# Output weights of the second layer split in halves, and two steps of waiting work behind each memory query

## The chip, the cores and the metric

The kernel runs on one core of one Trainium2 chip. The metric is the device time of one execution in microseconds; runs of the kernel before gave 899.07, 900.21 and 903.23 us, so the median is 900.21 us. A core has five engines that work side by side, each through its own list of instructions in a fixed order: TensorE (PE in the profile; its weight loads are PEld), VectorE (DVE), ScalarE (ACT), GpSimd (POOL) and SyncE (SP, which issues the loads). They wait for each other by semaphores. An instruction that waits holds up everything behind it on its engine.

## The reference

One inference step of a decoder trunk with two layers, for 256 prompt tokens and 8 single-token samples with shared weights (model width 2048). What matters for the second layer, cut down:

```
q, f, iv, mq, g = split(h @ w_in)            # 12 heads q/f/iv, 4 memory queries mq, 16 gate blocks g
fg  = lb + (1 - lb) * sigmoid(f)             # HGRN2: gated linear recurrence
o   = chunked_recurrence(silu(q), 1 - fg, iv, log(fg))   # per head, causal, with a state
mix = o * rsqrt(mean(o*o) + eps) * norm_w    # 12 blocks of 128
p   = softmax(mq @ mem_k.T / sqrt(128))      # 4 memory heads; prompt: one shared memory,
mem = p @ mem_v                              #   samples: each its own cached memory
y   = (concat(mix, mem) * silu(g)) @ w_out
out = layer_norm(alpha * h + y)
```

Everything is float32 at the interface.

## The kernel before

Each float32 operand of a large product is split into a high and a low float16 part, and a product is three matmuls (high x high, high x low, low x high; `passes`, L302 to L306). Activations lie transposed: 128 partitions of the width, 264 tokens in the free dimension (256 of the prompt, 8 samples).

All weights and cached memories pass through one **stream** (class `Stream`). A unit of the stream is a block of 128 x 2048 float32, 1 MB. Three things happen to it: SP loads it into one of 4 `raw` buffers (L80); `prep` splits it into one of 4 `hl` buffers, ACT writing the high part (L98) and DVE the low part (L99); then the unit's function runs its matmuls. Unit 4 onwards of the first layer's units is split in one piece of 2048 columns; units whose number is in `stream.halved` are split in two pieces of 1024, each with an instruction on ACT and one on DVE. In the kernel before, the set holds the 2048-column units of the second layer up to the last gate, and not the 16 blocks of output weights, which are added to the stream after it is computed.

Beside the units there is waiting work: generators in the queue `side`, run a step at a time by `pump`. After each unit the function `after` calls `pump(1)`. The last recurrence generator (`hg_side`, ten steps for a pair of heads) and then four memory-head generators (`memp_side`, two steps each) are in that queue while the second layer's last units pass: 4 memory queries (`mq`), then the samples' memory keys (`ck_unit`, 4 units) and values (`cv_unit`, 4 units) between the gate blocks `g`, then the 16 output blocks `o`.

The names that the texts use, with their lines:

- `rms` (L1183) is the last matmul of a recurrence head; ACT takes its logarithm and exponential (L1184, L1187, a table load before each), DVE then scales the head (L1190) and the gate follows (L729 on DVE, L730 on ACT, L731 on DVE). L734 and L735 make the gate itself from `g`.
- Memory heads of the prompt: scores `msc` (PE), maximum on DVE (L612, L613), exponential on ACT (L615), reciprocal and scaling on DVE (L616, L618), transposes `mpt` (L623 on PE), split into `mphl` (L250 on ACT for the high part, L252 on DVE for the low part), product `mpo` (PE), copy to `mix` (L635).
- Samples: score columns `mss` over the four `ck` units, then `mems_soft`: transposes `mrow` (L667 on PE), maximum (L671, L672 on DVE), exponential (L673 on ACT), reciprocal and scaling (L674, L675 on DVE), transposes `mback` (L678 on PE), split into `msphl` (L250 on ACT, L252 on DVE), and the products `mso` (L697, L698 on PE) over the four `cv` units.
- Output: `proj` into a PSUM bank `o`, residual L748 on DVE, square L760 on ACT, sums L765 and L766 on DVE. The last eight output blocks are split into `held` buffers of their own and are used twice: for 176 tokens first, for the other 88 at the end.

PSUM banks are shared by tag, two buffers each: `sc` for the scores and `rms`, `pt` for all transposes (`mpt`, `mrow`, `mback`), `pj` for gates and outputs. A buffer is given out anew when its last reader is through, in the order in which the program asks. The program asks for a bank when a generator's step or a unit runs, so `pump` also sets the order in which banks change hands. A scheduler then arranges the instructions of each engine; the result is a fixed order per engine.

Of the kernel before, what the change touches and what calls it, by code (L numbers as in the profile page):

```python
# [31 lines left out]
NM = 4  # L32
# [103 lines left out]
def trunk_kernel(  # L136
# [42 lines left out]
    stream = Stream(nc, cp, 4, 4)  # L179
# [34 lines left out]
    def small_work():  # L214
        with ExitStack() as behind:
            for first in (*stream.settled, first_mm[0]):
                behind.enter_context(tc.issue_after(first.ins))
            small_ops()
# [66 lines left out]
    def pump(n):  # L285
        for _ in range(n):
            while side:
                try:
                    next(side[0])
                    break  # L290
                except StopIteration:
                    side.popleft()
            if not side:
                return

    def drain():
        while side:
            for _ in side.popleft():
                pass
# [8 lines left out]
    def proj(hl, src, n, name, cols=slice(None), tag="pj"):  # L308
        w = hl.rearrange("p s (c f) -> p s c f", c=NC)
        pt = bank(tag, 2, name)  # L310
        for c in range(NC):
            passes(pt[:, :n], lambda s: w[:, s, c], lambda s: src[:, s, c, cols], c == 0, c == NC - 1)
        return pt[:, :n]
# [11 lines left out]
    def spread_bias(g):  # L325
        dst = bass.AP(tensor=l_d.tensor, offset=l_d.offset + g * 32 * 287, ap=[[LROW, 24], [288, 32], [1, 287]])
        src = l_t[:, 96 - 32 * g : 383 - 32 * g].unsqueeze(1).to_broadcast([24, 32, 287])
        nc.gpsimd.dma_start(dst, src)
# [47 lines left out]
    def v_rows(p):  # L376
        f = slice(p * P, (p + 1) * P)
        pt = bank("pt", 2, f"vt{p}")
        for n in range(2):
            nc.tensor.transpose(pt[:, n * P : (n + 1) * P], vf[:, p, n * P : (n + 1) * P], ident)  # L380
        nc.tensor.transpose(pt[:TS, 256:384], vf[:, p, TP:T], ident)
        src = pt[:, :256].rearrange("p (n f) -> p n f", n=2)
        split_from(vhl[:, 0, :, f], vhl[:, 1, :, f], src, SA)
        nc.vector.tensor_copy(vsn[:, f], pt[:TS, 256:384])
# [178 lines left out]
    def mq_unit(h):  # L563
        def fn(hl):
            pt = proj(hl, xhl, T, f"mq{h}")
            split_from(mqhl[:, 0, h], mqhl[:, 1, h], pt, 1.0 / SW)

        return fn
# [152 lines left out]
    def gate_fin(l):  # L721
        a, j = fin[l].popleft()
        while j not in done[l]:
            pump(1)
        assert (("swa" if l == 0 else j) if j < NQ else "mem") in done[l]
        gate_by(a, mix[:, j], j)
# [6 lines left out]
    def silu2(out, pt):  # L733
        nc.scalar.activation(out, pt, AF.Tanh, scale=0.5 * CP)  # L734
        nc.vector.scalar_tensor_tensor(out, out, 1.0, pt, op0=ALU.add, op1=ALU.mult)  # L735
# [4 lines left out]
    def out_part(l, i, hl, cols, tag="pj", first=False):  # L740
        n = len(range(*cols.indices(T)))
        pt = proj(hl, bhl, n, f"o{l}{i}_{cols.start}", cols, tag)
        with tc.high_priority(400) if first else nullcontext():
            residual(l, i, cols, n, pt)
# [23 lines left out]
    def out_unit(l, i):  # L768
        def fn(hl):
            if i == 0:  # L770
                drain()
                while fin[l]:
                    gate_fin(l)
                for s in range(2):
                    acc[s] = cp.tile([P, T], F32, tag="mphl", name=f"acc{l}{s}", bufs=2)
            if l == 0 or i < NC - NSPLIT:
                out_part(l, i, hl, slice(0, T))
            else:
                held[i] = hl
                out_part(l, i, hl, slice(0, TA))  # L780
            if i == NC - 1:
                if l == 0:
                    side.append(layer_norm())
                else:
                    finish_tokens()

        return fn
# [37 lines left out]
    def layer_norm():  # L825
        def homes(k):
            tags = ("mean", "sil", 3), ("rstd", "sil", 3), ("r0", "sq", 2)
            return [cp.tile([P, T], F32, tag=tag, name=f"{n}{k}", bufs=bufs) for n, tag, bufs in tags]

        mean, rstd = norm_factors(0, slice(0, T), homes)  # L830
        for i in range(NC):
            z = xres[:, i]
            w, b = ln_scalars(0, i)
            tc.keep_in_program_order(nc.vector.tensor_tensor(z, z, mean, op=ALU.subtract))
            tc.keep_in_program_order(nc.vector.scalar_tensor_tensor(z, z, w, rstd, op0=ALU.mult, op1=ALU.mult))
            nc.scalar.activation(z, z, AF.Identity, bias=b)
            split_from(xhl[:, 0, i], xhl[:, 1, i], z, SA)
            if i % 2 == 1:
                yield
        yield  # L840
# [70 lines left out]
    def wb(w, i):  # L911
        return w[i].rearrange("p c f -> p (c f)")
# [97 lines left out]
    def hq_unit(h):  # L1010
        def fn(hl):
            p1 = H["p"]
            pt = proj(hl, xhl, T, f"hq{h}")
            if h % 2 == 0:
                cur["q"] = p1.tile([P, 2, T], F32, tag="hq", name=f"hqs{h}", bufs=2)
            silu2(cur["q"][:, h % 2], pt)
            if h % 2 == 1:
                side.append(hg_side(h // 2, cur["q"], cur["vn"], cur["fg"], cur["qk"]))

        return fn  # L1020
# [31 lines left out]
    def early_gate(j):  # L1052
        def fn(hl):
            silu2(mix[:, j], proj(hl, xhl, T, f"g1{j}"))

        return fn
# [190 lines left out]
    n_first = len(stream.units)  # L1247
    for pi in range(HD // 2):
        for part, unit in (("f", f_unit), ("v", hv_unit)):
            for i in range(2):  # L1250
                stream.add(wb(w_in1, NB1[part] + 2 * pi + i), unit(2 * pi + i))
        for h in (2 * pi, 2 * pi + 1):
            stream.add(wb(w_in1, NB1["q"] + h), hq_unit(h))
            state_at[h] = len(stream.units)
            stream.add(state[pi][:, (h % 2) * TS * P : (h % 2 + 1) * TS * P], state_unit(h), SA, whole=True)
            if h < NG1:
                stream.add(wb(w_in1, NB1["g"] + h), early_gate(h))
    for h in range(NM):
        stream.add(wb(w_in1, NB1["mq"] + h), mq_unit(h))

# [6 lines left out]
    def g1(j):  # L1267
        stream.add(wb(w_in1, NB1["g"] + j), gate_unit(1, j))
# [5 lines left out]
            g1(late.popleft())  # L1274
    while late:
        g1(late.popleft())
    whole_w = {i for i in range(n_first, len(stream.units)) if stream.units[i][0].shape[1] == 2048}
    stream.halved = whole_w
    for i in range(NC):
        stream.add(wb(w_o[1], i), out_unit(1, i), home=hold if i >= NC - NSPLIT else None)  # L1280

    def after(i):
        if i == 1:
            small_work()
        if i == 4:
            for p in range(2):
                v_rows(p)
        if 1 <= i < 3:
            spread_bias(2 * i - 2)
            spread_bias(2 * i - 1)  # L1290
        pump(1)
        for rows in due:
            rows()
        due[:], later[:] = later, []

    stream.run(after)
    l2.close()

# [138 lines left out]
```

## Time and profile before

| what | us |
|---|---|
| median of 3 runs | 900.21 (899.07 to 903.23) |
| the profiled execution | 900.73 |
| its span (first to last instruction) | 898.9 |
| PE busy in the span | 884.6 (98%) |
| DVE busy | 703.3 (78%) |
| ACT busy | 587.7 (65%) |

How to read it: 1.8 us of the profiled execution's time lie around its span. A PE matmul's end is modelled: one of 264 columns is drawn with about 0.28 us, though the next starts 0.11 us later, so a real pause of PE looks some 0.17 us shorter in busy and idle times than it is between the starts of two matmuls. The second layer's part that the change touches begins with the four memory queries at about 710 us; the samples' memory lies between 732 and 780 us, the first output block starts at 792.7 us, the last weights are split at about 845 us.

### The profile page before, as it was taken

To read this page: it belongs to the slowest core of one execution; us is meant where nothing else is said; L and a number is where in the kernel's file an instruction comes from. 1 tells how busy PE (TensorE), PEld (TensorE's weight loads), DVE (VectorE), ACT (ScalarE), POOL (GpSimd) and SP (SyncE) were. 2 spreads that over 40 slices of the span, in tenths; PEclk is the share of its full clock that TensorE was granted. 3 is DMA by queue.
4 is the path that set the end of the run, shared out by engine and by line. 5 is a ranking of instruction groups with operands and counts; after the bars stand their busy time and mean duration, and the time that the engine had idled before them with its cause. 6 is when DMAs were issued, how large, how long until landed. Compare 5 with 4: busy or idle time off the path is not lost.

```text
span 898.9 us, 21938 instructions
## 1 busy us (share of the span) xinstructions
PE 884.6 (98%) x9281; PEld 761.1 (85%) x9281; DVE 703.3 (78%) x1294; ACT 587.7 (65%) x1046; POOL 34.9 (4%) x68
## 2 busy tenths in 40 slices
PE   9999999999999999999999999999999999999996
PEld 6888889678888888875888888888888988888896
DVE  7869877669886666697598798978879999878736
ACT  6757776657664433476767777768779676957415
POOL 1100010000000000002000000000000000000000
PEclk9999999999999999999999999999999999999999
DMA  9998566557795555556474553835446678666303
GB/s 348 385 355 320 191 244 201 188 209 270 253 333 204 200 187 191 192 207 223 148 273 152 214 212 130 307 134 217 178 183 233 238 279 302 227 234 253 124 2 98
DMA packets 37854, 198.68 MB, mean 221 GB/s; under 512 B 4555, under 2 KB 10732, under 8 KB 17532
## 3 DMA queue, kind: packets, MB, share of 16 engines
q1 hardware_dynamic: 33024, 181.55, 55.5%
q0 software_dynamic: 4688, 15.67, 4.6%
q8 instruction: 72, 1.18, 0.5%
q14 instruction: 26, 0.21, 0.1%
q10 hardware_dynamic: 44, 0.07, 0.1%
HBM read 180.03 MB, written 17.22 MB: 219 GB/s over the span
## 4 chain that ended last, share of the span: by engine, by line
PE 81%; DVE 11%; ACT 4%; issue 2%; DMA 1%; ACTq 0%; DVEq 0%
PE o L304 5%; PE o L306 5%; PE o L305 5%; PE g L304 5%; PE g L306 5%; PE g L305 5%; DVE hl L99 5%; PE q L304 2%; PE q L306 2%; PE q L305 2%; PE hv L304 2%; PE hv L306 2%; PE hv L305 2%; PE hq L305 2%; PE hq L304 2%
## 5 line engine op out<-in xcount | busy, mean ns | idle before, releaser
L99 DVE SCALAR_TENSOR_TENSOR hl<-raw,hl 128x1024 f16<-128x1024 f32 (+2 forms) x232 | 365.0, 1592 | 68.4 <-ACT hl L98 68.0
L98 ACT ACTIVATE hl<-raw 128x1024 f16<-128x1024 f32 (+2 forms) x232 | 305.0, 1344 | 87.8 <-PE o L306 47.0
L305 PEld LDWEIGHTS <-hl 128*128 128x128 f16 (+2 forms) x2048 | 197.3, 98 | 30.8 <-issue 2.5
L304 PEld LDWEIGHTS <-hl 128*128 128x128 f16 (+2 forms) x2048 | 197.4, 98 | 30.1 <-ACT xhl L250 1.2
L306 PEld LDWEIGHTS <-hl 128*128 128x128 f16 (+2 forms) x2048 | 197.3, 98 | 28.6 <-DVE hl L99 0.3
L306 PE MATMUL g<-xhl,hl 128*128 128x264 f16 x512 | 141.4, 276 | 0.0
L305 PE MATMUL g<-xhl,hl 128*128 128x264 f16 x512 | 141.4, 276 | 0.0
L304 PE MATMUL g<-xhl,hl 128*128 128x264 f16 x512 | 141.3, 276 | 0.0
L304 PE MATMUL o<-mix,hl 128*128 128x264 f16 x384 | 105.5, 276 | 2.2 <-DVE xres L748 1.8
L306 PE MATMUL o<-mix,hl 128*128 128x264 f16 x384 | 105.8, 276 | 0.0
L305 PE MATMUL o<-mix,hl 128*128 128x264 f16 x384 | 105.8, 276 | 0.0
L304 PE MATMUL q<-xhl,hl 128*128 128x264 f16 x192 | 53.0, 276 | 0.0
L304 PE MATMUL hv<-xhl,hl 128*128 128x264 f16 x192 | 53.0, 276 | 0.0
L305 PE MATMUL hq<-xhl,hl 128*128 128x264 f16 x192 | 53.0, 276 | 0.0
L306 PE MATMUL hq<-xhl,hl 128*128 128x264 f16 x192 | 53.0, 276 | 0.0
L304 PE MATMUL hq<-xhl,hl 128*128 128x264 f16 x192 | 53.0, 276 | 0.0
L305 PE MATMUL q<-xhl,hl 128*128 128x264 f16 x192 | 53.0, 276 | 0.0
L306 PE MATMUL hv<-xhl,hl 128*128 128x264 f16 x192 | 53.0, 276 | 0.0
L306 PE MATMUL q<-xhl,hl 128*128 128x264 f16 x192 | 53.0, 276 | 0.0
L305 PE MATMUL hv<-xhl,hl 128*128 128x264 f16 x192 | 53.0, 276 | 0.0
L305 PE MATMUL f<-xhl,hl 128*128 128x264 f16 x192 | 52.9, 276 | 0.0
L306 PE MATMUL f<-xhl,hl 128*128 128x264 f16 x192 | 52.8, 276 | 0.0
(338 smaller groups left out, 1856.1 us busy)
## 6 DMA issues: line engine op xcount, KB each, us to landing
raw<-in_w_in SPq DMA_DIRECT2D x88, 1024.0 KB, 5.6
raw<-in_w_o SPq DMA_DIRECT2D x32, 1024.0 KB, 4.8
raw<-in_w_mk SPq DMA_DIRECT2D x8, 1024.0 KB, 4.9
raw<-in_w_mv SPq DMA_DIRECT2D x8, 1024.0 KB, 4.9
raw<-in_c_mk SPq DMA_DIRECT2D x8, 1024.0 KB, 4.9
raw<-in_c_mv SPq DMA_DIRECT2D x8, 1024.0 KB, 4.9
raw<-in_state SPq DMA_DIRECT2D x12, 512.0 KB, 4.6
out_ss<-raw POOLq DMA_DIRECT2D x12, 512.0 KB, 2.9
```

Of the source, the lines that this page charges most:

```text
L98: hi = self.nc.scalar.activation(hl[:, 0, s], raw[:, s], AF.Copy, scale=scale)
L99: lo = self.nc.vector.scalar_tensor_tensor(hl[:, 1, s], raw[:, s], scale, hl[:, 0, s], op0=ALU.mult, op1=ALU.subtract)
L304: mm(out, lhs(0), rhs(0), start=start, stop=False)
L305: mm(out, lhs(0), rhs(1), start=False, stop=False)
L306: return mm(out, lhs(1), rhs(0), start=False, stop=stop)
```

## The change

Two edits. First, behind each of the four memory-query units of the second layer (`twos` holds their numbers) `pump` runs two steps of the waiting work where it ran one. Second, `stream.halved` is computed after the 16 output blocks have been added, so these are split in two pieces of 1024 columns as well.

```
+    twos = range(len(stream.units), len(stream.units) + NM)
     for h in range(NM):
         stream.add(wb(w_in1, NB1["mq"] + h), mq_unit(h))
...
-    whole_w = {i for i in range(n_first, len(stream.units)) if stream.units[i][0].shape[1] == 2048}
-    stream.halved = whole_w
     for i in range(NC):
         stream.add(wb(w_o[1], i), out_unit(1, i), home=hold if i >= NC - NSPLIT else None)
+    stream.halved = {i for i in range(n_first, len(stream.units)) if stream.units[i][0].shape[1] == 2048}
...
-        pump(1)
+        pump(2 if i in twos else 1)
```

What the scheduler makes of it stands below at three places. The first is PE around `mback`, the transposes that bring the samples' softmax back. Before, they stand in the middle of a gate block (the one for block 12 of the branch):

```order
L306 MATMUL g_10972<-xhl,hl_10762 128x264
L304 LDWEIGHTS hl_10762
L304 MATMUL g_10972<-xhl,hl_10762 128x264
L678 MATMUL mback_10814<-ident,mrows_10806 128x32 x2
L305 LDWEIGHTS hl_10762
L305 MATMUL g_10972<-xhl,hl_10762 128x264
L306 LDWEIGHTS hl_10762
```

Now (`mrow` stands 15 matmuls ahead of `mback`, right behind the third memory head's scores):

```order
L305 MATMUL mpo_10735<-mphl_10732,mvhl 128x256
L306 LDWEIGHTS mvhl
L306 MATMUL mpo_10735<-mphl_10732,mvhl 128x256
L678 MATMUL mback_10874<-ident,mrows_10866 128x32 x2
L623 MATMUL mpt_10880<-ident,ms_10806 128x128 x4
L697 LDWEIGHTS hl_10743
L697 MATMUL mso_10982<-msphl_10877,hl_10743 128x2
L698 LDWEIGHTS hl_10743
```

The gate blocks 11, 12 and 13 now all stand ahead of it on PE; behind it come all four units of sample values (`mso`) together with the rest of the memory heads, and then the gate blocks 14 and 15. Before, two of the values' units stood behind gate block 12 and two behind block 13. Between the last `rms` and the third head's scores `msc` PE now has 54 matmuls of gates and 12 of scores.

The second place is DVE behind the last recurrence heads. Before:

```order
L252 SCALAR_TENSOR_TENSOR msphl_10817<-mback_10814,msphl_10817 128x64
L1190 SCALAR_TENSOR_TENSOR mix<-osb_9824,small_t,osq_10758 128x264
L1190 SCALAR_TENSOR_TENSOR mix<-osb_9824,small_t,osq_10760 128x264
L612 TENSOR_REDUCE mnm_10894<-msc_10892 128x2
L729 SCALAR_TENSOR_TENSOR sil_10744<-sil_10744,mix 128x264
L729 SCALAR_TENSOR_TENSOR sil_10886<-sil_10886,mix 128x264
L613 TENSOR_SCALAR mnm_10894<-mnm_10894 128x2
L612 TENSOR_REDUCE mnm_11029<-msc_11027 128x2
```

Now, from the same heads up to the first two heads' maxima:

```order
L729 SCALAR_TENSOR_TENSOR sil_10952<-sil_10952,mix 128x264
L99 SCALAR_TENSOR_TENSOR hl_11031<-raw_10748,hl_11031 128x1024
L612 TENSOR_REDUCE mnm_10673<-msc_10671 128x2
L99 SCALAR_TENSOR_TENSOR hl_11031<-raw_10748,hl_11031 128x1024
L735 SCALAR_TENSOR_TENSOR sil_11087<-sil_11087,g_11038 128x264
L612 TENSOR_REDUCE mnm_10807<-msc_10805 128x2
L731 TENSOR_TENSOR mix<-sil_10799,mix 128x264
L731 TENSOR_TENSOR mix<-sil_10952,mix 128x264
L613 TENSOR_SCALAR mnm_10673<-mnm_10673 128x2
L613 TENSOR_SCALAR mnm_10807<-mnm_10807 128x2
```

and from there to the samples' split:

```order
L612 TENSOR_REDUCE mnm_11095<-msc_11093 128x2
L99 SCALAR_TENSOR_TENSOR hl_11110<-raw_10827,hl_11110 128x1024
L672 TENSOR_SCALAR mrnm_10867<-mrnm_10867 32x1
L99 SCALAR_TENSOR_TENSOR hl_11110<-raw_10827,hl_11110 128x1024
L735 SCALAR_TENSOR_TENSOR sil_11221<-sil_11221,g_11172 128x264
L613 TENSOR_SCALAR mnm_11095<-mnm_11095 128x2
L252 SCALAR_TENSOR_TENSOR mphl_10732<-mpt_10727,mphl_10732 128x512
L616 RECIPROCAL mz_10961<-mz_10961 128x2
L674 RECIPROCAL mrz_10868<-mrz_10868 32x1
L618 TENSOR_SCALAR ms_10959<-ms_10959,mz_10961 128x256 x2
L675 TENSOR_SCALAR mrows_10866<-mrows_10866,mrz_10868 32x256
L252 SCALAR_TENSOR_TENSOR msphl_10877<-mback_10874,msphl_10877 128x64
```

Before, the samples' split `msphl` is ahead of the last recurrence heads (L1190) on DVE, and with it the whole samples' softmax; now it is behind them and behind the first head's split `mphl`. Ahead of the first `mphl` now stand the splits of both remaining units of sample values (`hl_11031`, `hl_11110`).

The third place is DVE among the output blocks, at the residuals of the sixth and seventh block (L748). Before:

```order
L99 SCALAR_TENSOR_TENSOR held_11909<-raw_11672,held_11909 128x2048
L766 TENSOR_TENSOR acc_11438<-acc_11438,sq_0_11724 128x264
L99 SCALAR_TENSOR_TENSOR held_11968<-raw_11735,held_11968 128x2048
L748 SCALAR_TENSOR_TENSOR xres<-xres,o_0_11737 128x264
L99 SCALAR_TENSOR_TENSOR held_12025<-raw_11794,held_12025 128x2048
L765 TENSOR_TENSOR acc_11437<-acc_11437,xres 128x264
L748 SCALAR_TENSOR_TENSOR xres<-xres,o_0_11796 128x264
```

Now:

```order
L748 SCALAR_TENSOR_TENSOR xres<-xres,o_0_11755 128x264
L99 SCALAR_TENSOR_TENSOR held_12051<-raw_11814,held_12051 128x1024
L99 SCALAR_TENSOR_TENSOR held_12110<-raw_11875,held_12110 128x1024 x2
L765 TENSOR_TENSOR acc_11445<-acc_11445,xres 128x264
L766 TENSOR_TENSOR acc_11446<-acc_11446,sq_0_11805 128x264
L99 SCALAR_TENSOR_TENSOR held_12169<-raw_11936,held_12169 128x1024
L748 SCALAR_TENSOR_TENSOR xres<-xres,o_0_11816 128x264
```

The sixth block's residual (`o_0_11737`, now `o_0_11755`) stood behind the split of the fifth held block and now stands behind it and the first half of the sixth (`held_12051`); the seventh's stood behind the sixth held block and now stands behind the seventh and half of the eighth.

## The prediction

> **What bounds the kernel now.** I read the page's busy line and its chain of work first:
>
> ```profile
> span 898.9 us, 21938 instructions
> PE 884.6 (98%) x9281; PEld 761.1 (85%) x9281; DVE 703.3 (78%) x1294; ACT 587.7 (65%) x1046; POOL 34.9 (4%) x68
> PE 81%; DVE 11%; ACT 4%; issue 2%; DMA 1%; ACTq 0%; DVEq 0%
> ```
>
> TensorE is the bound: busy for 98% of the span, and 81% of the chain that ended last. No matmul is added or taken away, so the change can win only time in which PE pauses, and can lose only by new pauses. The next view, busy time by stage, says how much there is to win. I cut it where the chain of waits has its steps on other engines:
>
> ```profile
> 720.00:770.00 50.00, 49.71 (x620) 43.81 (x618) 43.60 (x70) 36.73 (x55) 0.54 (x1) 1.00 0.78 289
> 784.00:798.00 14.00, 14.00 (x127) 12.36 (x126) 14.00 (x21) 9.21 (x18) 0.00 (x0) 1.00 0.88 343
> 798.00:802.00 4.00, 3.17 (x26) 2.22 (x24) 3.61 (x9) 2.78 (x8) 0.00 (x0) 1.00 0.77 256
> 834.00:838.00 4.00, 2.24 (x27) 1.90 (x25) 4.00 (x5) 2.24 (x2) 0.00 (x0) 1.00 0.98 393
> 838.00:890.00 52.00, 52.00 (x823) 50.91 (x821) 28.68 (x70) 18.14 (x45) 0.00 (x0) 1.00 0.10 32
> 890.00:898.90 8.90, 1.49 (x6) 0.61 (x4) 4.03 (x12) 2.98 (x9) 1.65 (x4) 0.88 0.28 96
> ```
>
> After the length of the stage come PE, its weight loads, DVE, ACT and GpSimd, then the granted clock. PE has two pauses that the change could reach, one at 798 to 802 us (0.83 us idle) and one at 834 to 838 us (1.76 us idle). DVE is busy 14.00 of 14.00 us just ahead of the first and 4.00 of 4.00 around the second: where PE waits, it waits for a DVE that is full. The timeline of PE shows the true size of the first pause:
>
> ```profile
> 798.07 0.28 PE L305 MATMUL o<-mix,hl 128*128 128x264 f16 x1
> 798.18 0.28 PE L306 MATMUL o<-mix,hl 128*128 128x264 f16 x1
> 798.48 0.27 PE L304 MATMUL mpo<-mphl,mvhl 128*128 128x256 f16 x1
> 799.21 0.27 PE L304 MATMUL o<-mix,hl 128*128 128x264 f16 x1 [0.45 <-ACT mix L730]
> 799.70 0.27 PE L305 MATMUL mpo<-mphl,mvhl 128*128 128x256 f16 x1 [0.22 <-DVE mphl L252]
> ...
> 800.46 0.28 PE L304 MATMUL o<-mix,hl 128*128 128x264 f16 x1
> 800.87 0.27 PE L304 MATMUL mpo<-mphl,mvhl 128*128 128x256 f16 x1
> ```
>
> Two starts of undisturbed matmuls lie 0.11 us apart (798.07, 798.18). What exceeds that is 0.19 + 0.62 + 0.38 + 0.30 = 1.5 us: the memory heads' last transposes and splits are late when the first output block begins. For the second pause DVE and PE read:
>
> ```profile
> 834.52 2.29 DVE L99 SCALAR_TENSOR_TENSOR held<-raw,held 128x2048 f16<-128x2048 f32 x1
> 836.73 0.43 DVE L748 SCALAR_TENSOR_TENSOR xres<-xres,o 128x264 f32<-128x264 f32 x1
> 837.20 0.27 PE L304 MATMUL o<-mix,hl 128*128 128x264 f16 x1 [1.76 <-DVE xres L748]
> ```
>
> PE's eighth output block waits for a PSUM bank, which the sixth block's residual (L748) frees, and that stood behind a 2.29 us split. Everything that the change can win is thus 1.5 + 1.9 us, or 3.4 us of 900.
>
> **The moved work.** The order shows that the two extra steps move more than themselves. The memory heads now ask for their PSUM banks ahead of the samples' softmax, and so `mrow`, `mback` and all of `mso` fall behind the heads' scores and the first split. PE's list between the last `rms` and the third head's scores holds only gates and scores, and behind them a row of small steps, each of which goes to DVE and ACT and back. I lay that stretch out by hand, with the durations of the stage 755 to 805 us:
>
> ```profile
> L99 DVE SCALAR_TENSOR_TENSOR hl<-raw,hl 128x1024 f16<-128x1024 f32 x15 | 17.8, 1223 | 0.4 <-ACT hl L98 0.4
> L731 DVE TENSOR_TENSOR mix<-sil,mix 128x264 f16<-128x264 f32 x7 | 2.9, 433 | 1.0 <-ACT mix L730 1.0
> L252 DVE SCALAR_TENSOR_TENSOR mphl<-mpt,mphl 128x512 f16<-128x512 f32 x4 | 2.8, 693 | 0.0
> L612 DVE TENSOR_REDUCE mnm<-msc 128x2 f32<-128x512 f32 x4 | 2.7, 685 | 0.0
> L735 DVE SCALAR_TENSOR_TENSOR sil<-sil,g 128x264 f32<-128x264 f32 x6 | 2.5, 425 | 0.0
> L618 DVE TENSOR_SCALAR ms<-ms,mz 128x256 f32<-128x256 f32 x8 | 2.4, 351 | 0.0
> L1190 DVE SCALAR_TENSOR_TENSOR mix<-osb,small_t,osq 128x264 f32<-128x264 f32 x2 | 0.9, 489 | 4.1 <-ACT osq L1187 4.1
> L613 DVE TENSOR_SCALAR mnm<-mnm 128x2 f32<-128x2 f32 x4 | 0.7, 165 | 0.0
> L671 DVE TENSOR_REDUCE mrnm<-mrow 32x1 f32<-32x256 f32 x1 | 0.4, 403 | 0.0
> L675 DVE TENSOR_SCALAR mrows<-mrows,mrz 32x256 f32<-32x256 f32 x1 | 0.3, 342 | 0.0
> ...
> L98 ACT ACTIVATE hl<-raw 128x1024 f16<-128x1024 f32 x14 | 14.0, 1047 | 0.0
> L615 ACT ACTIVATE ms<-msc,mnm 128x256 f32<-128x256 f32 x8 | 3.7, 473 | 0.3 <-DVE mnm L613 0.3
> L250 ACT ACTIVATE mphl<-mpt 128x512 f16<-128x512 f32 x4 | 2.4, 589 | 0.0
> L734 ACT ACTIVATE sil<-g 128x264 f32<-128x264 f32 x5 | 1.9, 380 | 0.1
> L615 ACT ACTIVATION_READ_ACCUMULATOR ms<-msc,mnm 128x1 f32 x8 | 1.7, 207 | 0.0
> ```
>
> The means are full lengths; back to back an instruction starts before the last one ends, as three splits show:
>
> ```profile
> 757.89 3.50 DVE L99 SCALAR_TENSOR_TENSOR hl<-raw,hl 128x1024 f16<-128x1024 f32 x3
> 767.94 0.61 PE L1183 MATMUL rms<-osq,ones_rms 128*128 128x264 f32 x2
> 770.84 0.90 DVE L1190 SCALAR_TENSOR_TENSOR mix<-osb,small_t,osq 128x264 f32<-128x264 f32 x2 [4.11 <-ACT osq L1187]
> ```
>
> (3.50 - 1.22) / 2 = 1.14, so I take 0.09 us off each that has a follower. L729 is of L731's form and gets its length; L616, L672 and L674 are of L613's size.
>
> *First wait, third head's scores.* They need the `sc` bank of the first head, which ACT's exponential frees. From the second `rms` to L1190 on DVE it takes 770.84 - 767.94 = 2.90 us, and ACT's steps between them are the same now. Then DVE's rows as they now stand: L1190 twice 0.80, L729 twice 0.68, L99 1.14, L612 0.60, L99 1.14, L735 0.34, L612 0.60, L731 twice 0.68, L613 twice 0.25: 6.2 us. The first head's two exponentials with their read-outs are 0.47 + 0.21 twice, less four overlaps, about 1.0. Sum 10.1 us behind `rms`. PE has meanwhile the two passes of `rms` (0.44 us), 54 gate and 12 score matmuls at 0.11 us: 7.7 us. PE waits **2.4 us**.
>
> *Second, the first head's product, high part.* Call the start of the third scores T. PE has 18 small matmuls to the first `mpo`: T + 2.0. ACT has the second head's exponentials 1.0, two splits 1.9, L734 0.3 and L250 0.6: T + 3.7. PE waits **1.7 us**.
>
> *Third, its low part on DVE.* DVE has the third head's maximum at T + 0.9 (six score matmuls and a handover), and then L612 0.60, L616 0.07, L671 0.31, L613 0.08, L618 twice 0.52, L612 0.60, L99 1.14, L672 0.07, L99 1.14, L735 0.34, L613 0.08, L252 0.69: T + 6.5. PE was let go at T + 3.7 for one matmul: it waits **2.7 us**.
>
> *The rest.* DVE then has 1.0 us up to L675 (L616, L674, L618 twice, L675), PE 0.55 us of `mpo`: 0.45 us at `mback`. The split of `mback` on both engines has only four transposes as cover: 0.4 us. The second and third heads' splits come each behind a pair of weight splits for gate blocks 14 and 15, with the values' matmuls as cover: from 0 to 1.1 us, I take 0.7. Together **1.55 us**.
>
> New pauses: 2.4 + 1.7 + 2.7 + 1.55 = 8.35 us. Bounds: if the two pieces of L99 in the first wait and the two in the third were ready to run elsewhere, each wait would be 2.3 us shorter and 8.35 become 3.7; if each of the five handovers between engines costs 0.4 us more than I allow, it is 10.35.
>
> What goes: the 1.5 us at 798 us, since the memory heads are through before gate block 14. This stage is 8.35 - 1.5 = +6.85 us. Behind the stalled instructions on PE stand the two last gates and all output blocks, so nothing else can fill the time. The loads of the values' units and of gates 14 and 15 cost nothing more: SP issues them as buffers come free, and they have these 8 us in addition. If that cover were gone, a late 1 MB load would show as a wait of ACT's L98 for DMA.
>
> **The split output weights.** DVE: three halves in a row give 1.14 for each that has a follower, so a block takes 2 x 1.14 instead of 2.29 - 0.09 = 2.20, or 0.08 us more, 1.3 us for 16 blocks, spread over the 50 us of the output stage in which DVE has gaps. The halves let DVE begin one half earlier behind ACT and put a residual between two halves. But in the new order the sixth residual stands behind half a split more than before, and the seventh behind one and a half more. Take the sixth: without new loads' delay it comes 1.14 us later by the longer row and about 1 us earlier because ACT's and DVE's halves overlap. Bounds: the whole 1.9 us at 834 us goes, or a second wait of the same size comes at the next bank, +1.9. The rows are nearest to no change; I take 0.
>
> The page "Perfetto Trace Analysis" of the Trainium skill, section "Optimizing Scalar/DVE Operations", says that larger operations help where such an engine is saturated, and that breaking instructions up lets work be done sooner where it is not saturated but holds up others. By its second half the 1.9 us would go and the sum be 4.95; by its first, with DVE full for 4.00 of 4.00 us here, nothing is won.
>
> **Sum.** 6.85 + 0 on the profiled execution's span of 898.9 us gives 905.75, with the 1.83 us around it 907.6 us. That execution was 0.5 us above the median; on the median the forecast is 900.21 + 6.85 = **907.1 us**.
>
> **The rivals.**
>
> *The stretch stays hidden (not slower).* The place is the first wait. It decides when DVE's stretch from L1190 to the last L613 is shorter than what PE has: 6.2 must fall under 7.7 - 2.9 - 1.0 = 3.8 us. If the splits of the values' unit ran in the 4.1 us in which DVE idled ahead of L1190 (its row says so), 2.3 us would leave the stretch, the first wait would be near 0 and the second and third begin 2.3 us earlier. In the same way the third would lose its 2.3. What is left of the second and the rest are about 2.0 us of new pauses, if the high part's two splits are done early as well, against 1.5 to 3.4 gone: 898.8 to 900.7 us, say 899.8. For it: the idle 4.1 us are there. Against: the new order puts L99 behind L1190 on DVE, and an engine does not overtake.
>
> *Half of it.* One of the two pairs of splits is out of the way or the output stage gains its 1.9 us: 907.1 - 2.3 to 907.1 - 4.2, about 903.5 us. For it: the pause at 834 us is one of DVE's granularity. Against: the residuals' places.
>
> *The clock falls.* In the second and third wait together PE would do one matmul in 4.5 us. A lower granted clock is seen in the last row by stage (0.88 with PE busy 1.49 of 8.90 us) and not at 834 to 838 us (1.00 with 2.24 of 4.00). If it falls here, the matmuls that follow take twice their 0.11 us. With 0.88 over 8.9 us some 2.1 us were at half clock there; the 48 matmuls of a gate block would pay up to 5.3 us. The time would be 908 to 912 us, say 910. The page "TensorE: Matmul & The Clock Gate" of the Trainium skill, section "Part 1: The HAM clock gate (the "warmup" mystery)", puts the fall at one idle window of about 3.4 us, and my third wait alone is shorter than that; second and third together are longer, with a matmul between them.
>
> *The output stage pays too.* A second bank wait of 1.9 us, and none of the first gone: 907.1 + 1.9 = 909.0 us. For it: both residuals stand further back. Against: halves let ACT and DVE overlap more.
>
> **How the numbers follow.** The forecast's mechanism, with 3.7 to 10.35 us of new pauses less 1.5 at the outside, has 0.68; half of it 0.13; hidden 0.09; the clock 0.05; the output stage as well 0.05. Its own range is 903.5 to 909.2 us. The likeliest is 907.1. For 8 of 10 I reach down into the second rival and up into the last two: 902.0 to 910.0 us. What a measurement can tell from no change is about 0.5%, here 4.5 us: 895.7 to 904.7. Slower than that: of the 0.68 some 0.59, all of the last two, a fifth of the half case, 0.72 together. Faster by over 4.5 us would need more than the 3.4 us that are there: 0.03. No difference: 0.25.
>
> **What would show it.** Right: in the profile after, PE's waits name `msc`, `mpo` (high part from ACT, low part from DVE) and `mback`, in sum 6 to 9 us between 765 and 795 us, and nothing at the first output block; DVE shows L99 between the first head's L612 and L613. The first output block begins about 7 us later than 792.7. The stage of the last ten blocks is as before, DVE full, a bank wait of 0 to 3 us at a residual. Wrong: PE busy throughout the stretch; the samples' softmax waiting for nothing; a granted clock under 1.00 in it; or a pause of over 4 us among the output blocks, which would say that loads, not the row on DVE, set that stage.

## The result and the profile after

The changed kernel takes 909.43 us (median of 4 runs, 908.59 to 909.87), the kernel before 899.83 us on the same chips: a ratio of 1.0107, 95% interval 1.0093 to 1.0122, so 9.6 us slower. The forecast was 907.1 us with a range of 902.0 to 910.0. The page of its profiled execution (909.87 us):

```profile
span 908.1 us, 21972 instructions
PE 890.3 (98%) x9281; PEld 765.2 (84%) x9281; DVE 705.9 (78%) x1310; ACT 590.3 (65%) x1062; POOL 35.0 (4%) x68
PE 86%; DVE 8%; ACT 4%; issue 1%; ACTq 0%
```

PE is drawn busy 890.3 us instead of 884.6, with the same 9281 matmuls. That cannot be waiting, since waiting is not busy: some matmuls ran longer. Busy time by stage shows which (columns as in the prediction; the granted clock is the third number from the end):

```profile
765.00:775.00 10.00, 10.00 (x88) 8.56 (x86) 5.03 (x9) 7.39 (x13) 0.00 (x0) 1.00 0.44 161
775.00:785.00 10.00, 4.54 (x25) 3.17 (x23) 7.95 (x22) 6.18 (x18) 0.00 (x0) 0.80 0.31 105
785.00:795.00 10.00, 9.72 (x138) 8.13 (x138) 7.48 (x16) 7.66 (x15) 0.00 (x0) 0.50 0.41 131
795.00:805.00 10.00, 10.00 (x98) 8.32 (x97) 8.88 (x14) 6.81 (x12) 0.00 (x0) 0.84 0.99 383
835.00:845.00 10.00, 10.00 (x92) 8.70 (x91) 10.00 (x13) 8.10 (x9) 0.00 (x0) 1.00 0.98 385
```

Three things are to be seen. From 775 to 785 us PE does 25 matmuls in 10 us: the new waits. From 777 to 798 us the granted clock is at half for much of the time (0.80, 0.50, 0.84): the rival to which I gave 0.05. And at 835 us, where PE had paused 1.76 us before, it is busy throughout with DVE just as full. The waits in PE's timeline:

```profile
775.31 0.28 PE L306 MATMUL g<-xhl,hl 128*128 128x264 f16 x1
777.81 0.37 PE L304 MATMUL msc<-mkhl,mqhl 128*128 128x256 f16 x1 [2.22 <-ACT ms L615]
777.97 0.42 PE L305 MATMUL msc<-mkhl,mqhl 128*128 128x256 f16 x1
778.19 0.42 PE L306 MATMUL msc<-mkhl,mqhl 128*128 128x256 f16 x1
782.18 0.27 PE L304 MATMUL mpo<-mphl,mvhl 128*128 128x256 f16 x1 [0.69 <-ACT mphl L250]
785.27 0.37 PE L305 MATMUL mpo<-mphl,mvhl 128*128 128x256 f16 x1 [2.83 <-DVE mphl L252]
```

They stand where the hand replay put them, third scores, first product, its low part, and name ACT, ACT and DVE as forecast. Measured from start to start, less 0.11 us for the matmul itself, they are 2.39, 0.85 and 2.99 us; 0.24 us follow at `mback`. And score matmuls now start 0.21 us apart (777.97, 778.19), where the same ones start 0.11 us apart in the kernel before. DVE's timeline in the same stretch is the row that the prediction added up:

```profile
770.49 0.90 DVE L1190 SCALAR_TENSOR_TENSOR mix<-osb,small_t,osq 128x264 f32<-128x264 f32 x2 [4.97 <-ACT osq L1187]
771.99 1.22 DVE L99 SCALAR_TENSOR_TENSOR hl<-raw,hl 128x1024 f16<-128x1024 f32 x1
773.73 1.21 DVE L99 SCALAR_TENSOR_TENSOR hl<-raw,hl 128x1024 f16<-128x1024 f32 x1
776.49 0.23 DVE L613 TENSOR_SCALAR mnm<-mnm 128x2 f32<-128x2 f32 x2
...
781.81 1.21 DVE L99 SCALAR_TENSOR_TENSOR hl<-raw,hl 128x1024 f16<-128x1024 f32 x1
783.01 1.20 DVE L99 SCALAR_TENSOR_TENSOR hl<-raw,hl 128x1024 f16<-128x1024 f32 x1
784.55 0.67 DVE L252 SCALAR_TENSOR_TENSOR mphl<-mpt,mphl 128x512 f16<-128x512 f32 x1
```

From L1190 to the last L613 it is 776.72 - 770.49 = 6.23 us; I had 6.2. While DVE waited 4.97 us ahead of it, the pieces of L99 stood behind it in DVE's order. The first output block starts at 808.25 us.

**One thing about the comparisons.** The first 100 us differ by chance from one execution to the next, in instructions that all these kernels have in common: the first memory query of the second layer starts between 702.9 and 705.7 us in the profiles (703.6 in the kernel before, not at about 710 as the text ahead of the prediction has it), and the timed runs of the kernel before alone go from 898.1 to 903.2 us. So beside the medians I compare, in each profile, the stretch from the first memory query to the end of the span: 195.29 us before, 204.48 us after, 9.19 us more.

### The profile page after: what moved, and what is told of

It reads as the page before. It is cut to its first block, busy times and chain, and to the rows that moved or that the text cites. A ratio compares the mean times of both kernels' runs of the same rounds, so it can differ in the third digit from the quotient of the medians.

```text
span 908.1 us, 21972 instructions
## 1 busy us (share of the span) xinstructions
PE 890.3 (98%) x9281; PEld 765.2 (84%) x9281; DVE 705.9 (78%) x1310; ACT 590.3 (65%) x1062; POOL 35.0 (4%) x68
## 4 chain that ended last, share of the span: by engine, by line
PE 86%; DVE 8%; ACT 4%; issue 1%; ACTq 0%
PE o L306 6%; PE o L304 6%; PE o L305 6%; PE g L304 6%; PE g L305 5%; PE g L306 5%; DVE hl L99 4%; PE q L306 2%; PE q L304 2%; PE q L305 2%; PE hv L306 2%; PE hv L305 2%; PE hv L304 2%; PE hq L305 2%; PE hq L304 2%; PE hq L306 2%
## 5 line engine op out<-in xcount | busy, mean ns | idle before, releaser
L99 DVE SCALAR_TENSOR_TENSOR hl<-raw,hl 128x1024 f16<-128x1024 f32 (+2 forms) x240 | 365.1, 1540 | 67.9 <-ACT hl L98 67.0
```

Of the source, the lines that this page charges most:

```text
L99: lo = self.nc.vector.scalar_tensor_tensor(hl[:, 1, s], raw[:, s], scale, hl[:, 0, s], op0=ALU.mult, op1=ALU.subtract)
```

## The experiments

The table has all runs. "Rest" is that stretch, from one profile each. Each ratio is to runs of the kernel before on the same chip; their medians lie between 899.38 and 900.21 us.

| kernel | median us | ratio to before (95% interval) | rest, us |
|---|---|---|---|
| before | 899.83 | | 195.29 |
| after | 909.43 | 1.0107 (1.0093 to 1.0122) | 204.48 |
| halves alone | 900.56 | 1.0012 (1.0001 to 1.0023) | 193.82 |
| halves alone, again | 899.72 | 0.9996 (0.9982 to 1.0009) | 194.59 |
| two steps alone | 909.19 | 1.0113 (1.0096 to 1.0130) | 203.81 |
| softmax in another bank | 899.70 | 1.0001 (0.9990 to 1.0011) | 193.94 |
| matmuls in the waits | 908.53 | 1.0102 (1.0079 to 1.0124) | 200.79 |
| two extra steps | 899.23 | 0.9992 (0.9980 to 1.0005) | 193.97 |
| three extra steps | 910.45 | 1.0108 (1.0087 to 1.0128) | 204.53 |
| four low pieces left out | 906.52 | 1.0065 (1.0047 to 1.0082) | 200.50 |
| wide matmuls among narrow | 909.85 | 1.0110 (1.0089 to 1.0132) | 204.57 |

**The halves alone.**

```
-        pump(2 if i in twos else 1)
+        pump(1)
```

> Only the output weights are split in halves; one step of waiting work behind every memory query, as before. First theory (the moved steps carry the whole loss, and the halves by themselves end the 1.9 us bank wait among the output blocks): 899.8 - 1.9 = 897.9 us, the stretch from 760 to 800 us as before, no wait on the residual. Second reading (that wait went only because the output blocks began later and found their splits done): 899.8 us, with the wait still there. Rival (the halves carry part of the loss through a fuller DVE): 902 us or more.

The loss is gone. The rest is 1.5 us shorter than before, and the wait on the residual has shrunk from 1.8 to 0.2 us (waits of PE, total us, times, longest):

```profile
PE o L304 <- DVE xres L748: 0.2, 1, 0.2
```

The median does not show it: 900.56 us. In the profile the first memory query came 2.07 us later than before; whether the other runs began late too is not known, since they left no profile. So the same kernel ran again:

> The kernel with the halves alone once more. In its first profile it took 193.8 us from the first memory query to the end (before: 195.3) but 2.1 us more up to the first memory query, in instructions that are the same as before. If that late start was chance: about 898 us and 0.9985 of the time before. If it comes with this kernel: 900.5 us again, with the first memory query at about 705.7 us.

This time the first memory query came at 703.0 us, so the late start was chance. The rest was 0.7 us shorter than before, and the median, 899.72 us, missed the 898 that I expected. The residual's wait is not gone but smaller by an amount that varies:

```profile
PE o L304 <- DVE xres L748: 0.7, 1, 0.7
```

In both profiles a wait of 0.5 us at `mpt` (L623, on DVE's L618) has come in, which the kernel before doesn't have. The halves are worth 0.7 to 1.5 us in the profiles, and nothing that the medians can tell.

**The two steps alone.** The set of halved units is computed ahead of the output blocks, as in the kernel before:

```
+    whole_w = {i for i in range(n_first, len(stream.units)) if stream.units[i][0].shape[1] == 2048}
+    stream.halved = whole_w
     for i in range(NC):
         stream.add(wb(w_o[1], i), out_unit(1, i), home=hold if i >= NC - NSPLIT else None)
-    stream.halved = {i for i in range(n_first, len(stream.units)) if stream.units[i][0].shape[1] == 2048}
```

> Only the two steps behind each memory query; output weights split in one piece. First theory: the waits at the third head's scores (2.4 us), at the first head's product (0.8 and 3.0 us) and the half clock behind them stay as in the changed kernel; 909.4 us if the later start of the output blocks had removed the 1.9 us bank wait, 911.3 us if the halves had. Rival (the halves carry part of the loss): 906 us or less.

909.19 us, the whole loss. PE's waits:

```profile
PE mpo L305 <- DVE mphl L252: 2.7, 1, 2.7
PE msc L304 <- ACT ms L615: 2.2, 1, 2.2
PE mpo L304 <- ACT mphl L250: 1.4, 1, 1.4
```

There is no wait on L748 here either, though the output weights are split in one piece. So the moved steps alone end that wait too, and the halves alone shorten it. The likely reason here is that the output blocks begin 14.5 us later and find more of their splits done; no run shows that by itself.

The granted clock fell only once here ahead of the tail, at 783.74 us. Busy time of PE in the three stretches ahead of that (then clock, DMA share and GB/s):

```profile
773.50:776.91 3.41, 1.76 (x16) 1.00 0.35 82
776.91:780.32 3.41, 2.18 (x18) 1.00 0.54 226
780.32:783.74 3.42, 0.27 (x1) 1.00 0.00 0
```

It stayed up behind the first wait, fell behind the second and third together, and was at half for 13.65 us.

**The samples' softmax in another bank.** Both edits stay; `mrow` and `mback` go into free columns of the bank in which the samples' scores stand (in both layers).

```
-        pr = bank("pt", 2, f"mrow{l}")
+        pr = mst["s"][:, 128:384]
...
-        pb = bank("pt", 2, f"mback{l}")
+        pb = mst["s"][:, 384:]
```

> The changed kernel, with mrow and mback written into free columns of the bank of the samples' scores (mss), so that the samples' softmax needs no bank of the transposes. First theory (the order in which banks were asked for put the samples' softmax, and with it all of the samples' values, behind the heads' scores): the softmax is early again, the values' units stand among gates 12 and 13, no wait over 1 us and a granted clock of 1.00 between 770 and 790 us; about 898 to 900.5 us. Rival (the row on DVE is too long whatever the banks do, since two steps more have to be done in the same stretch): 904 to 909 us with waits on DVE at the heads' products.

899.70 us; no loss. The stages from 770 us, and the line of `mback` (which here writes into `mss`):

```profile
770.00:780.00 10.00, 10.00 (x149) 8.88 (x147) 6.56 (x12) 9.22 (x14) 0.00 (x0) 1.00 0.30 107
780.00:790.00 10.00, 9.67 (x130) 8.62 (x127) 10.00 (x20) 9.23 (x19) 0.00 (x0) 1.00 0.83 315
```
```profile
767.60 0.31 PE L678 MATMUL mss<-ident,mrows 32*128 32x32 f32 x2
```

In the changed kernel L678 ran at 786.43 us. With the same steps run at the same units, taking the softmax out of the heads' queue for banks puts it back into the gates and the loss is gone. So the cause is not that more steps are done, but that the heads' transposes and the softmax share two buffers, given out in the order of asking.

**Matmuls in the waits.** 58 matmuls of 256 columns, whose results nobody reads, at the three places where PE waits.

They stand behind the gate for block 13, behind the first head's transposes, and behind the high part of its product:

```
-            pt = proj(hl, xhl, T, f"g{l}{j}")
+            pt = proj(hl, xhl, T, f"g{l}{j}"); l == 1 and j == 13 and fill(18)
...
-        po = bank("pv", 1, f"mpo{l}{h}")
+        po = bank("pv", 1, f"mpo{l}{h}"); l == 1 and h == 0 and fill_behind(tr, 14, po)
...
-                m == 1,
+                m == 1, (26, po, False) if (l, h, m) == (1, 0, 0) else 0,
```

> The changed kernel plus 58 matmuls of 256 columns on operands at hand whose results nobody reads: 18 behind gate 13, 14 ahead of the first head's product, 26 between its high and its low part, that is where PE waits. Theory of the clock (the waits let the granted clock fall to half for 17 us, and the matmuls done at half clock cost some 4 us beside the waits): PE is never idle long enough, the clock stays at 1.00 up to 788 us or longer, the waits' ends stay where DVE and ACT put them, and 58 more matmuls make it faster: about 905.2 us (904 to 907). Rival (half clock costs nothing, since it falls into waits): 909.4 us. Rival (the added matmuls delay the chain): 911 us or more.

In the profile the rest falls from 204.48 to 200.79 us, 3.7 us less with 58 matmuls more, and the clock stays at 1.00 up to the tail of the span:

```profile
776.64 2.13 PE L603 MATMUL mss<-mkhl 128*128 128x256 f16 x18
779.03 0.27 PE L304 MATMUL msc<-mkhl,mqhl 128*128 128x256 f16 x1 [0.25 <-ACT ms L615]
781.05 1.69 PE L603 MATMUL mpo<-mkhl 128*128 128x256 f16 x14
782.71 3.00 PE L603 MATMUL mpo<-mkhl 128*128 128x256 f16 x26
787.71 0.28 PE L678 MATMUL mback<-ident,mrows 32*128 32x32 f32 x2 [1.20 <-DVE mrows L675]
```
```profile
780.00:790.00 10.00, 8.69 (x105) 7.45 (x103) 7.83 (x20) 5.90 (x18) 0.00 (x0) 1.00 0.32 113
```

The six runs fall into two groups. In three the mean granted clock of the span was 0.997 or 0.998, with spans of 903.9, 905.6 and 905.6 us; in three it was 0.992 or 0.993, with 907.8, 909.4 and 910.4 us. In the second group the clock must have fallen somewhere; these runs left no trace, so where is not shown. The groups lie 4.2 us apart, of the same size as the 3.7 us between the profiles (the start's 2 us of chance is in it). The median, 908.53 us, mixes both and is no measure of either. It lies outside the 904 to 907 us that I expected; the profiled run (907.5 us, with its first memory query 1.2 us later than in the kernel before) is near its upper end.

**Two and three extra steps.**

```
-    twos = range(len(stream.units), len(stream.units) + NM)
+    twos = {len(stream.units) + k for k in (0, 1)}
```

and with (0, 1, 2) for three.

> The changed kernel with two steps behind the first two memory queries alone (two extra steps in all; halves kept). Theory of the order of requests: with two extra steps the samples' softmax still asks for its bank of transposes ahead of the first head's transposes (mrow, mback, then mpt), so nothing is lost in the stretch 770 to 790 us: 195.3 us from the first memory query to the end in the kernel before become about 194, and the time about 898 us. Theory of a price per step (each extra step moves some 2.3 us of the 9 us): about 904.5 us.

> The changed kernel with two steps behind the first three memory queries (three extra steps; halves kept). Theory of the order of requests: the third extra step is the one that puts the first head's transposes ahead of the samples' softmax, so the whole loss is there at once: 909 us, the waits of 2.4, some 1 and 3 us as in the changed kernel. Theory of a price per step: about 906.8 us.

899.23 and 910.45 us: nothing, and everything. The rests are 193.97 and 204.53 us. The numbers in the tiles' names give the order in which the program asks. With two extra steps it is msc_10772, mrow_10830, mback_10841, mpt_10847: the first head's scores come ahead of the softmax, its transposes behind, and L678 runs at 764.6 us as in the kernel before. With three it is msc_10710, mpt_10789, mrow_10846, mback_10857: the transposes have gone ahead, and the waits are there:

```profile
764.62 0.31 PE L678 MATMUL mback<-ident,mrows 32*128 32x32 f32 x2
```
```profile
PE mpo L305 <- DVE mphl L252: 2.5, 1, 2.5
PE msc L304 <- ACT ms L615: 2.2, 1, 2.2
PE mpo L304 <- ACT mphl L250: 0.7, 1, 0.7
```

A price per step is refuted; it is one request that changes places. The rest with two extra steps is as short as those of the other bank and of the first run of the halves, but 0.9992 (0.9980 to 1.0005) is no gain that can be told from none.

**Four low pieces left out.** L99 of the last two units of sample values isn't run; `mso` takes their high part twice, so the low part of these values is left out of the product.

```
-            lo = self.nc.vector.scalar_tensor_tensor(
+            lo = i in self.bare or self.nc.vector.scalar_tensor_tensor(
...
-                        mm(ov[:, h, b, 0:1], v[:, 1, bb, m, f], phl[:, m, r, 0:1], start=False, stop=m == 1)
+                        mm(ov[:, h, b, 0:1], v[:, 0 if l and t > 1 else 1, bb, m, f], phl[:, m, r, 0:1], start=False, stop=m == 1)
...
```

> The changed kernel with the low part of the samples' values left out in their last two units (the four pieces of L99 that stand in the two waits; the product takes the high part twice instead, so PE has as many matmuls). First theory (the row on DVE with these four pieces in it sets the waits): the first wait falls from 2.4 to about 0.2 us, the one at the low part of the first head's product from 3.0 to about 0.8, the row 3.8 us shorter in all; 905.6 us if the clock falls as before, 901 to 902 us if the shorter waits keep it up. Rival (DVE waits for its inputs, so less work on it moves nothing): 909.4 us.

```profile
779.98 0.27 PE L304 MATMUL mpo<-mphl,mvhl 128*128 128x256 f16 x1 [1.39 <-ACT mphl L250]
780.83 0.27 PE L305 MATMUL mpo<-mphl,mvhl 128*128 128x256 f16 x1 [0.57 <-DVE mphl L252]
782.28 0.28 PE L678 MATMUL mback<-ident,mrows 32*128 32x32 f32 x2 [0.74 <-DVE mrows L675]
```

The first wait is down to 0.16 us from start to start, the low part's to 0.73: each 2.2 us shorter, the two pieces of L99 that stood in it (2.28 us). The row on DVE sets these two waits. The high part's wait grew from 0.85 to 1.55 us and `mback` has one of 0.9, so not all of it is won. The rest is 4.0 us shorter; the clock fell all the same, for 13.65 us, and 906.52 us is nearest to the case "as before" (905.6).

**Wide matmuls among the narrow ones.** 20 matmuls of 256 columns behind the first unit of sample values, to see what brings the clock back.

```
-            ov = mst["o"][:, :64].rearrange("p (h b s) -> p h b s", h=NM, s=2)
+            ov = mst["o"][:, :64].rearrange("p (h b s) -> p h b s", h=NM, s=2); (l, t) == (1, 1) and [mm(mst["o"][:, 128 : 128 + TP], mkhl[:, 0, 0, :P], mkhl[:, 0, 1], start=True, stop=True) for _ in range(20)]
```

> The changed kernel plus 20 matmuls of 256 columns (results unread) among the samples' values, behind the first unit's mso products. In the changed kernel the granted clock stayed at half for 13.65 us, 784.45 to 798.11, although PE is drawn busy all that time, mostly with products of 1 and 2 columns. Theory that narrow products do not bring the clock back: the wide ones, some 4 us of work at half clock, do, and it rises one or two periods of 3.41 us earlier; the time stays near 909 us, as the added work eats what the clock gives back. Rival (after such a fall the clock stays low for a fixed 13.65 us): it rises after four periods again, and the time is 911 to 913 us.

By itself this run doesn't decide. The clock fell at 778.15 us, behind the first wait, and was up again at 791.80, after four periods of 3.41 us, as the rival has it. The moment fits the first theory: 16 of the 20 wide matmuls started between 788.09 and 791.51 us, and the gate's matmuls, with which the clock had risen in the changed kernel, came only at 796.28. That a low clock always lasts 13.65 us is refuted by the changed kernel and the one with three extra steps, whose first falls lasted 3.41 us; all five other falls ahead of the tail did last 13.65. 909.85 us, and not the rival's 911 to 913: the added work ate what it gave.

## Why the prediction was right, and where it was wrong

**The moved work: right in place, order and sum.** In the kernel with the filled waits, at full clock, the new waits can be counted without the clock: 58 matmuls of 0.109 us (1.69 - 0.27 over 13) are 6.3 us, and about 2 us of pauses are left, together 8.4 us. The sum was 8.35. Counted there from start to start, added matmuls included, the single terms are: first wait 2.39 us (forecast 2.4); the product's high part 1.55 (1.7; at most, since PE doesn't wait behind the added matmuls there); its low part 3.1 (2.7); `mback` 1.36, where I had 0.45 there and 1.55 with the splits behind it. In the changed kernel they are 2.39, 0.85, 2.99 and 0.24: the second and the last are smaller because half-clock matmuls stood in their place. The bound by the pieces of L99 was tested: taking the four out made the two waits 2.2 us shorter each (I had 2.3).

One sign was off: I had the first output block about 7 us later, and it is 15.5 us later (792.72 to 808.25). In the kernel before, 26 matmuls of the memory heads, some 2.8 us, and the 1.5 us of pauses lay behind that start; now they are ahead of it or gone.

**What goes: right.** The four pauses at the first output block, 1.5 us, are gone, and about 0.5 us of small ones at 764 and 780 us besides, which I hadn't counted.

**The clock: wrong.** I gave it 0.05, and the forecast has no term for it. The rival had the place and the price nearly right: the longer fall, 13.65 of the 17.07 us at half clock, came behind the second and third wait, and its 910 us is nearer to the measured 909.43 than my 907.1. What failed is the chance I gave it, and that I did not ask what the 2.4 us of the first wait would do alone: behind it the clock fell for 3.41 us as well. Counted by the pitch of the same forms in the kernel before, 56 matmuls at half clock took 5.5 us longer. Some 2 us of that lay where PE would have waited anyway (8.4 us of waits at full clock are 6.5 here), so the net cost is some 3.5 us; the kernel with the filled waits gives 3.7.

**The split output weights: the size was off.** I took 0 between -1.9 and +1.9. The wait at 834 us went altogether, -1.9 us, with another 0.15 at 829; by the two steps alone it goes as well, so in the changed kernel it would be gone without the halves. The argument by rows on DVE (a half more ahead of the sixth residual) was beside the point: by itself the splitting takes 1.1 to 1.6 us off this wait, and 0.7 to 1.5 us off the rest. The page "Perfetto Trace Analysis" of the Trainium skill, section "Optimizing Scalar/DVE Operations", has larger operations for a saturated engine and smaller ones for one that is not saturated but holds up others. The traces are nearer to the second, though DVE was full for 4.00 of 4.00 us; the medians tell neither.

**Not seen:** an earlier recurrence step waits 0.7 us for ACT's L1080 at 736 us; all pauses of that stretch together are some 0.5 us more than before.

Together: 6.5 of waits + 5.5 of half clock + 0.5 - 1.5 - 0.5 - 2.1 = 8.4 of the 9.2 us between the profiles; the other 0.8 us are not accounted for. That 6.85 us came near 9.2 is in part chance: a term of 3.5 to 3.7 was missing and one of -1.9 too. The range holds the result only because it was drawn up into the last two rivals. By the bounds of the forecast's own sum (3.7 to 10.35, less 1.5) it reaches from 902.4 to 909.1 us; the 903.5 given as its lower end doesn't follow from them, and the measured 909.43 lies just above the upper one.

**The rivals.** "Hidden" fell with the first wait: DVE idled 4.97 us ahead of L1190, and L99 stood behind it. "Half of it" by a gain of the output stage: that gain came, but didn't halve anything. "The output stage pays too": no bank wait at all. Of what should have shown the forecast wrong, one thing came true, the clock under 1.00 in the stretch.

## What to carry to other kernels

Where small work shares a rotating set of PSUM buffers, count in which order the program asks for them, not only how many steps run: one request that changes places with another (the third extra step here, not the second) moved four units of work behind a row on another engine and cost some 10 us at once (rests of 193.97 and 204.53 us), and another home for two small tiles made the same steps free. And price a wait of TensorE of more than 2 us by two terms, the wait and the slower clock that may follow it; here they were 6.5 us of waits and 5.5 us of slower matmuls.

## What the runs showed of the hardware

**The granted clock goes by periods of 3.41 us, and in these profiles it fell behind each one in which PE was drawn busy for 1.37 us or less, and behind none with 1.60 us or more.** The records of the changed kernel change at 777.63, 781.04, 784.45 and 798.11 us: 3.41, 3.41 and four times 3.41 us apart. Cut at these moments, busy time (PE alone, then clock, DMA share and GB/s) reads:

```profile
774.21:777.63 3.42, 1.37 (x13) 1.00 0.48 122
777.63:781.04 3.41, 3.23 (x16) 0.50 0.44 185
781.04:784.45 3.41, 0.72 (x5) 1.00 0.00 0
784.45:787.87 3.42, 2.60 (x17) 0.50 0.74 263
787.87:791.28 3.41, 3.41 (x61) 0.50 0.13 48
791.28:794.69 3.41, 3.41 (x67) 0.50 0.26 38
794.69:798.11 3.42, 3.42 (x38) 0.50 0.97 359
798.11:801.52 3.41, 3.41 (x33) 1.00 0.97 368
```

After a period with 1.37 us busy the clock fell; so it did in the kernels with three extra steps, four pieces left out and wide matmuls after these:

```profile
776.47:779.88 3.41, 1.18 (x12) 1.00 0.64 219
```
```profile
779.08:782.49 3.41, 1.19 (x9) 1.00 0.63 223
```
```profile
774.73:778.15 3.42, 1.20 (x12) 1.00 0.74 280
```

It stayed up after 1.76 us in the kernel with the two steps alone (shown there). In the kernel before it stayed up after 1.65 us around the wait at 835 us and after 1.60 us near the end, if the periods are counted back from the fall at 896.72 us:

```profile
835.28:838.69 3.41, 1.65 (x19) 1.00 0.92 365
889.89:893.30 3.41, 1.60 (x6) 1.00 0.15 50
```

Counted so, the other profiles agree: the bound lies between 1.37 and 1.60 us of drawn busy time in a period, 40 to 47% of it. The wait of 2.39 us cost the clock in the changed kernel and the wait of the same length didn't in the kernel with the two steps alone, by where it fell in the periods. The page "TensorE: Matmul & The Clock Gate" of the Trainium skill, section "Part 1: The HAM clock gate (the "warmup" mystery)", gives such a free-running window of 3413 ns; the trace agrees to the nanosecond of its records (3413 and 13653 ns). The same section of that page of the Trainium skill has the clock fall after at least one idle window; here the window need not be idle: 1.37 us of work in it were not enough to keep the clock.

**Narrow products seem not to bring it back.** From 787.87 to 794.69 us PE is drawn busy all the time, with 128 matmuls of which most have 1 or 2 columns, and the clock stays at half; it rises after the first period that is mostly gate matmuls (794.69 to 798.11). The run with wide matmuls put among the narrow ones agrees in the moment of the rise and by itself doesn't settle it, since its other periods differ as well. All five profiles with falls ahead of the tail say more. For each of the 22 periods at half clock I added up the time that all matmuls but the narrow ones (L697, L698) took, from start to next start, at most 0.23 us each. Seven periods were followed by a rise, and these have 2.78 to 3.45 us of such matmuls; the other fifteen have 1.03 to 2.51 us, though PE was drawn busy for all 3.41 us in ten of them. That is in accord with the theory in every period, and the falls of 13.65 us then need no fixed length. A run that changes nothing but the width is missing.
